# Sample attention in a two-layer encoder step: scores and values of two samples in one TensorE visit, new-key products last

## The chip, the core and the metric

The kernel runs on one core of one Trainium2 chip. The metric is the device time of one execution in microseconds (us); of several executions the median counts. Engines are named as the profile names them: PE is TensorE, PEld its weight loads, DVE is VectorE, ACT is ScalarE, POOL is GpSimd, SP is SyncE (here only a queue that issues transfers).

## What is computed

A two-layer trunk runs over 640 frames of width 1024: 512 frames of one prompt and 8 running samples of 16 new frames each. Each layer is a feed-forward half step, a mixer, and another feed-forward half step; all matrix products are in 32-bit accuracy. The mixer projects to convolution, attention and gate columns and joins two branches. The part that matters here is the attention of the samples: each of the 8 samples has 16 queries, 256 cached keys and 16 new ones, in 8 heads of 64.

```python
def _sample_attention(q, k, v, ck, cv, rel_bias):
    k_all = jnp.concatenate([ck, k], axis=1)
    v_all = jnp.concatenate([cv, v], axis=1)
    ...
    out = _band_attention(q, k_all, v_all, q_pos, k_pos, rel_bias)

def _band_attention(q, k, v, q_pos, k_pos, rel_bias):
    s = jnp.einsum('bqhd,bkhd->bhqk', q, k).astype(jnp.float32) * (HEAD_DIM ** -0.5)
    s = s + rel_bias[:, idx].astype(jnp.float32)[None]
    ...
    p = jax.nn.softmax(s, axis=-1).astype(v.dtype)
    return jnp.einsum('bhqk,bkhd->bqhd', p, v)
```

## The kernel before, in words

**The order of work on TensorE in a mixer is written out by hand.** `attention` (L1569) first makes the values of all frames, then queries and keys of a head pair. From there on the rest of the projection is a stream of steps (`work`, L1601): three more query/key pairs, the convolution columns, and the first pair of gate columns. `fill(n)` (L1606) takes the next n steps of that stream. A step is six products of 128 weights by 320 frames (`block`, L389, called in halves by `seven`, L698); fourteen steps make one pair of column blocks, and they use up four weight slabs. The attention's own products are put between such steps, so that TensorE has projection products to do while other engines work on the attention. One such insertion is called a visit here. The prompt's attention comes first (`scores`, L1646, `values`, L1689), then the samples'. On VectorE, ScalarE, GpSimd and the DMA queues the compiler's scheduler orders the instructions; those inside `soon()` (L365) get a higher priority.

**Weights** come in loads of 512 KB on SyncE's queue (L245). Each slab is split into a high part by ScalarE (`whi`, L305) and a low part by VectorE (`wlo`, L310), some slabs after sums of two blocks (L249), about two slabs ahead of TensorE. There are three buffers each of raw weights, high and low parts.

**Scores of a sample** (`sscores`, L1740): the cached keys are loaded in two halves (L1746, 256 KB each) and the cached values in one piece (L1749, 512 KB); GpSimd adds the new keys behind the cached ones (L1754). Four products (L1757), one for a pair of heads, put the scores into the four 32-row strips of one PSUM bank `spss`. They contract over 128 rows and yield 32 rows by 272 keys; the trace lists each product as two records with shape 128*32. VectorE adds the bias and takes the maximum into the tile `box` (L1764, tile `ss` in the trace), and `softmax` (L1821) negates the maximum on VectorE, takes exponentials on ScalarE and the reciprocal on VectorE.

**Values of a sample** (`svalues`, L1772) go in three parts. First, three transposes turn the weights, two of 128 columns for the cached keys and one of 16 columns for the new keys (L1780, L1781, bank `sptp`); ScalarE and VectorE copy them back into `box` (L1783, L1784). Second, the products with the values (L1791, bank `spy`): four with the 16 new keys (shape 16*32), then eight with the cached ones (128*32), each listed as two records; ScalarE scales the result into `box` (L1793). Third, one transpose turns the result into a shared bank `ptx` (L1797); when four samples are in it (`G = 4`), VectorE and ScalarE copy it out (L1803).

**Buffers.** `box`, the loaded keys, the loaded values and the new values have two buffers each, so those of sample b + 2 come free when sample b is through with them: keys after its scores, values after its value products, `box` after its result's turn. The PSUM banks of the attention are four (`att`, L209); the projection's own are four others.

**The loop over samples** (L1807 to L1819): scores of samples 0 and 1 in one visit; then for each sample 4 steps, the weights' turn, 3 steps, the scores of sample b + 2 and right behind them the values of sample b in one visit, 2 steps, the result's turn. That is 72 steps, all that the stream has left, and what follows is the next stage.

Of the kernel before, what the change touches and what calls it, by code (L numbers as in the profile page):

```python
# [12 lines left out]
AF = mybir.ActivationFunctionType  # L13
# [3 lines left out]
P = 128  # L17
D = 1024
L = 2
SEQ = 512  # L20
NB = 8
TS = 16
T = SEQ + NB * TS
HT = T // 2
PAST = 256
H = 8
HD = 64
# [153 lines left out]
def trunk(ctx: ExitStack, tc: tile.TileContext, xin, wst, small, pbias, samplebias, kcache, vcache,  # L181
          yout, ko, vo, co):
    nc = tc.nc
    PE, DVE, ACT, POOL, SP = nc.tensor, nc.vector, nc.scalar, nc.gpsimd, nc.sync
# [8 lines left out]
    ps = ExitStack()  # L193
# [15 lines left out]
    def att(name):  # L209
        return banks["att"].tile([P, 512], F32, tag="att", name=name)  # L210
# [15 lines left out]
    for kind, inside in kinds():  # L226
        n = len(fourth)
# [137 lines left out]
    def soon():  # L365
        return tc.high_priority(offset=300)
# [34 lines left out]
    ident = cp.tile([P, P], F32, name="ident")  # L401
# [12 lines left out]
    for k in range(KT):  # L414
# [4 lines left out]
        if k % 2 == 0:  # L419
            c = slice(k * P, (k + 2) * P)  # L420
# [693 lines left out]
    def mixer(l, after):  # L1114
        with tc.tile_pool(name=f"yp{l}", bufs=1, reuse_waits="tile") as yp, \
# [19 lines left out]
            with tc.tile_pool(name=f"mp{l}", bufs=2, reuse_waits="tile") as mp:  # L1135
# [63 lines left out]
                with tc.manual_schedule(engines={mybir.EngineType.PE}):  # L1199
                    attention(l, h, st, stats, ops, mp, yas, ycp, both, others())  # L1200
# [368 lines left out]
    def attention(l, h, norms, stats, ops, mp, yas, ycp, both, others):  # L1569
# [3 lines left out]
        npair = H // 2  # L1573
        nt = T // P
        NQ = SEQ // P
        KS = PAST + TS
# [29 lines left out]
        def fill(n):  # L1606
            for _ in range(n):
                next(stream, None)
# [5 lines left out]
        for c in range(KT // 2):  # L1614
            wh, wl = chunk()
            for kk in range(2):
# [3 lines left out]
                for t in range(nt):  # L1620
                    for j, (w, xx) in enumerate(((wh, xh), (wh, xl), (wl, xh))):
                        PE.matmul(pv[t], xx[:, t * P : (t + 1) * P],  # L1622
                                  w[:, kk * AW : (kk + 1) * AW],
                                  start=c == 0 and kk == 0 and j == 0,
                                  stop=c == KT // 2 - 1 and kk == 1 and j == 2)
# [63 lines left out]
        def values(p):  # L1689

            pt = [mp.tile([P, offs[-1] + SEQ], F32, name=f"pt{l}_{2 * p + e}", tag="pt") for e in range(2)]
            at = [sum(P * (NQ - i) for i in range(j)) for j in range(NQ)]

            def turn(j, e):
                w = (NQ - j) * P
                s = weights[2 * p + e]
                ptp = att(f"ptp{l}_{2 * p + e}_{j}")[:, :w]
                for i in range(j, NQ):
                    PE.transpose(ptp[:, (i - j) * P : (i - j + 1) * P],
                                 s[:, offs[i] + j * P : offs[i] + (j + 1) * P], ident)  # L1700
                with soon():
                    (ACT.copy if e else DVE.tensor_copy)(pt[e][:, at[j] : at[j] + w], ptp)

            for j in range(NQ):
                for e in range(2):
                    turn(j, e)
                if j % 2:
                    yield
            py = att(f"py{l}_{p}")
            for j in range(NQ):  # L1710
                for e in range(2):
                    hh = 2 * p + e
                    PE.matmul(py[e * HD : (e + 1) * HD, j * P :], vs[j][:, hh * HD : (hh + 1) * HD],
                              pt[e][:, at[j] : at[j] + (NQ - j) * P], start=j == 0, stop=j == NQ - 1)
            ACT.copy(yas[:, p, 0:SEQ], py)
            yield
# [5 lines left out]
        for p in range(npair):  # L1722
# [3 lines left out]
            vals = values(p)  # L1726
# [7 lines left out]

        sbias = mp.tile([P, KS], F32, name=f"sbias{l}", bufs=1)
        POOL.dma_start(sbias, samplebias[l])
        G = 4
        held, ptx = {}, [None]

        def sscores(b):  # L1740
            n = f"{l}_{b}"
            kcs = []
            for e, tag in enumerate("qk"):
                kc = mp.tile([P, T], F32, name=f"kc{n}_{e}", tag=tag)
                kcs.append(kc[:, : npair // 2 * KS].rearrange("p (a k) -> p a k", k=KS))
                SP.dma_start(kcs[e][:, :, :PAST], kcache[l, b, :, e * npair // 2 : (e + 1) * npair // 2])  # L1746
            vraw = mp.tile([P, offs[-1] + SEQ], F32, name=f"vc{n}", tag="s")
            vraw = vraw[:, : 2 * AW].rearrange("p (a k) -> p a k", a=2)
            SP.dma_start(vraw, vcache[l, b])  # L1749
            rows = slice(b * TS, (b + 1) * TS)  # L1750
            vn = mp.tile([P, SEQ], F32, name=f"vn{n}", tag="bias")[:TS, :AW]
            SP.dma_start(vn, vnew[rows])
            for e, kc in enumerate(kcs):
                POOL.tensor_copy(kc[:, :, PAST:], ks[:, e * npair // 2 : (e + 1) * npair // 2, rows])  # L1754
            pss = att(f"spss{n}")[:, :KS]
            for p in range(npair):
                PE.matmul(pss[32 * p : 32 * p + 32], bd[:, b, p, :], kcs[2 * p // npair][:, p % (npair // 2), :],  # L1757
                          start=True, stop=True)

            box = mp.tile([P, offs[-1] + SEQ], F32, name=f"ss{n}", tag="pt")  # L1760
            s = box[:, :KS]
            st = mp.tile([P, 4, NQ], F32, name=f"sst{n}", tag="st", bufs=4)
            with soon():
                DVE.tensor_tensor_reduce(out=s, in0=pss, in1=sbias, scale=1.0, scalar=NEG,  # L1764
                                         op0=ALU.add, op1=ALU.max, accum_out=st[:, 0, 0:1])

                softmax(s, st, [(0, KS)])
                if b == NB - 1:
                    ACT.activation(early, st[:, 3, 0:1], AF.Sigmoid)
            held[b] = box, st, vraw, vn  # L1770

        def svalues(b):  # L1772
            n = f"{l}_{b}"
            box, st, vraw, vn = held[b]
            s = box[:, :KS]
            pt = box[:, KS : KS + 2 * P].rearrange("p (a b) -> p a b", a=2)
            pn, yx = (box[:n, KS + o * P : KS + (o + 1) * P] for n, o in ((TS, 2), (P, 3)))
            ptp = att(f"sptp{n}")
            for j in range(2):
                PE.transpose(ptp[:, j * P : (j + 1) * P], s[:, j * P : (j + 1) * P], ident)  # L1780
            PE.transpose(ptp[:TS, 2 * P : 3 * P], s[:, PAST:], ident)  # L1781
            with soon():
                ACT.copy(pt, ptp[:, : 2 * P].rearrange("p (a b) -> p a b", a=2))  # L1783
                DVE.tensor_copy(pn, ptp[:TS, 2 * P : 3 * P])  # L1784
            yield

            pys = att(f"spy{n}")[:, :P]
            for j, (w, v) in enumerate(((pn, vn), (pt[:, 0], vraw[:, 0]), (pt[:, 1], vraw[:, 1]))):
                for p in range(npair):
                    r = slice(32 * p, 32 * p + 32)  # L1790
                    PE.matmul(pys[r], w[:, r], v[:, p * P : (p + 1) * P], start=j == 0, stop=j == 2)  # L1791
            with soon():
                ACT.activation(yx, pys, AF.Copy, scale=st[:, 3, 0:1])  # L1793
            yield
            if b % G == 0:
                ptx[0] = att(f"ptx{n}")
            PE.transpose(ptx[0][:, (b % G) * P : (b % G + 1) * P], yx, ident)  # L1797
            if b % G == G - 1:
                c0 = SEQ + (b + 1 - G) * TS
                for e in range(2):  # L1800
                    r = slice(e * HD, (e + 1) * HD)
                    with soon():
                        (ACT.copy if e else DVE.tensor_copy)(  # L1803
                            yas[r, :, c0 : c0 + G * TS].rearrange("p a (b t) -> p a b t", b=G),
                            ptx[0][r].rearrange("p (b a e t) -> p a b e t", b=G, a=npair, e=2)[:, :, :, e, :])

        sscores(0)  # L1807
        sscores(1)
        for b in range(NB):
            vals = svalues(b)  # L1810
            fill(4)
            next(vals)
            fill(3)
            if b + 2 < NB:
                sscores(b + 2)
            next(vals)
            fill(2)
            next(vals, None)
        fill(KT * KT)  # L1819

    def softmax(s, st, parts):  # L1821


        n = len(parts)
        with soon():
            DVE.tensor_scalar(out=st[:, 1, :n], in0=st[:, 0, :n], scalar1=-1.0, scalar2=None, op0=ALU.mult)
        for i, (o, w) in enumerate(parts):
            ACT.activation(s[:, o : o + w], s[:, o : o + w], AF.Exp, bias=st[:, 1, i : i + 1],
                           accum_out=st[:, 2, i : i + 1])
        with soon():  # L1830
            DVE.reciprocal(st[:, 3, :n], st[:, 2, :n])
# [294 lines left out]
```

## Time and profile before

| | us |
|---|---|
| median of 3 runs | 2496.21 |
| lowest and highest | 2496.2 and 2496.61 |
| the profiled execution | 2496.66 |
| its span, first to last instruction | 2494.7 |
| sample stage of layer 0, first scores to last result's turn | 562.07 to 642.63 |
| the same of layer 1 | 1795.10 to 1875.72 |

The mean granted TensorE clock is 0.998 of full speed. The sample stages are some 81 us each, so both together are 6% of the span. The page's first part gives busy time and share of the span by engine, its second part the span in 40 slices; the timeline gives single instructions with start and length. A record's length on TensorE contains its way through the array, so records overlap, and the pace is read from start to start.

### The profile page before, as it was taken

To read this page: it belongs to the slowest core of one execution; us is meant where nothing else is said; L and a number is where in the kernel's file an instruction comes from. 1 tells how busy PE (TensorE), PEld (TensorE's weight loads), DVE (VectorE), ACT (ScalarE), POOL (GpSimd) and SP (SyncE) were. 2 spreads that over 40 slices of the span, in tenths; PEclk is the share of its full clock that TensorE was granted. 3 is DMA by queue.
4 is the path that set the end of the run, shared out by engine and by line. 5 is a ranking of instruction groups with operands and counts; after the bars stand their busy time and mean duration, and the time that the engine had idled before them with its cause. 6 is when DMAs were issued, how large, how long until landed. Compare 5 with 4: busy or idle time off the path is not lost.

```text
span 2494.7 us, 43515 instructions
## 1 busy us (share of the span) xinstructions
PE 2478.1 (99%) x17048; PEld 2419.0 (97%) x17048; DVE 2119.2 (85%) x3322; ACT 1450.0 (58%) x2343; POOL 370.7 (15%) x445
## 2 busy tenths in 40 slices
PE   9999999999999999999999999999999999999998
PEld 8999999888999999999999999998899999999998
DVE  7888888878888899888798889888788888989887
ACT  7455556674666555555565555556646665555554
POOL 0011211211111011111001111221111110111111
PEclk9999999999999999999999999999999999999999
DMA  4245665335345344655435555643344553455554
GB/s 146 82 107 124 138 135 130 106 115 167 99 119 145 101 116 118 138 135 135 117 90 126 129 134 123 138 119 115 125 153 104 126 141 95 119 133 122 129 135 110
DMA packets 133261, 308.10 MB, mean 124 GB/s; under 512 B 12768, under 2 KB 76128, under 8 KB 133056
## 3 DMA queue, kind: packets, MB, share of 16 engines
q1 hardware_dynamic: 68976, 219.18, 27.3%
q0 software_dynamic: 63360, 85.50, 20.6%
q8 instruction: 133, 2.18, 0.4%
q10 hardware_dynamic: 720, 0.65, 0.1%
q14 instruction: 72, 0.59, 0.1%
HBM read 221.13 MB, written 7.94 MB: 92 GB/s over the span
## 4 chain that ended last, share of the span: by engine, by line
PE 94%; DVE 3%; ACT 2%; DMA 1%; issue 0%; SPq 0%; DVEq 0%; ACTq 0%
PE pab L395 12%; PE paa L395 11%; PE pcb L395 6%; PE pca L395 6%; PE daa L962 5%; PE dab L962 5%; PE po L372 4%; PE qa L395 4%; PE pbb L395 3%; PE pba L395 3%; PE dca L962 3%; PE dcb L962 3%; PE pda L372 2%; PE pv L1622 2%; PE ma_cv L395 2%; PE qc L395 2%
## 5 line engine op out<-in xcount | busy, mean ns | idle before, releaser
L310 DVE TENSOR_TENSOR wlo<-raw,whi 128x512 fp32r<-128x512 f32 (+1 forms) x583 | 598.6, 1030 | 236.1 <-ACT whi L305 230.6
L305 ACT CAST whi<-raw 128x512 fp32r<-128x512 f32 (+1 forms) x583 | 519.9, 897 | 348.0 <-PE pbb L395 44.6
L305 ACT CAST whi<-s 128x1024 fp32r<-128x1024 f32 (+1 forms) x164 | 153.6, 937 | 248.1 <-issue 107.8
L395 PE MATMUL pab<-xhib,whi 128*128 128x320 f32 x704 | 218.3, 310 | 0.4 <-DVE gb L249 0.4
L395 PE MATMUL pab<-xhib,wlo 128*128 128x320 f32 x704 | 217.4, 309 | 0.0
L395 PE MATMUL pab<-xlob,whi 128*128 128x320 f32 x704 | 217.4, 309 | 0.0
L395 PE MATMUL paa<-xhia,whi 128*128 128x320 f32 x640 | 198.0, 309 | 0.2 <-DVE ga L249 0.2
L395 PE MATMUL paa<-xloa,whi 128*128 128x320 f32 x640 | 197.6, 309 | 0.0
L395 PE MATMUL paa<-xhia,wlo 128*128 128x320 f32 x640 | 197.6, 309 | 0.0
L310 DVE TENSOR_TENSOR wlo<-s,whi 128x1024 fp32r<-128x1024 f32 (+1 forms) x164 | 176.6, 1077 | 10.4 <-ACT whi L305 10.4
L395 PEld LDWEIGHTS pab<-xhib,whi 128*128 128x128 f32 x704 | 132.2, 188 | 1.1 <-DVE gb L249 0.9
L395 PEld LDWEIGHTS pab<-xlob,whi 128*128 128x128 f32 x704 | 132.2, 188 | 0.2
L395 PEld LDWEIGHTS pab<-xhib,wlo 128*128 128x128 f32 x704 | 132.2, 188 | 0.0
L395 PEld LDWEIGHTS paa<-xhia,whi 128*128 128x128 f32 x640 | 120.2, 188 | 0.5 <-DVE ga L249 0.5
L395 PEld LDWEIGHTS paa<-xloa,whi 128*128 128x128 f32 x640 | 120.2, 188 | 0.1
L395 PEld LDWEIGHTS paa<-xhia,wlo 128*128 128x128 f32 x640 | 120.2, 188 | 0.0
L249 DVE TENSOR_TENSOR raw<-raw,raw 128x512 f32<-128x512 f32 x164 | 112.2, 684 | 1.8 <-DMA raw<-in_wst 0.2
L249 DVE TENSOR_TENSOR raw<-s,raw 128x512 f32<-128x512 f32 x164 | 112.3, 685 | 0.0
L395 PE MATMUL pcb<-xhib,whi 128*128 128x320 f32 x352 | 108.7, 309 | 0.0
L395 PE MATMUL pcb<-xlob,whi 128*128 128x320 f32 x352 | 108.7, 309 | 0.0
L395 PE MATMUL pcb<-xhib,wlo 128*128 128x320 f32 x352 | 108.7, 309 | 0.0
L986 POOL DMA_DIRECT2D x<-c_b x52 | 62.6, 1203 | 309.5 <-ACT c_b L979 134.5
(816 smaller groups left out, 8170.8 us busy)
## 6 DMA issues: line engine op xcount, KB each, us to landing
raw<-in_wst SPq DMA_DIRECT2D x375, 512.0 KB, 3.7
x<-c_b POOLq DMA_DIRECT2D x52, 320.0 KB, 5.1
x<-c_a POOLq DMA_DIRECT2D x50, 320.0 KB, 5.0
kc<-in_kcache SPq DMA_DIRECT2D x32, 256.0 KB, 4.1
vc<-in_vcache SPq DMA_DIRECT2D x16, 512.0 KB, 4.5
ub<-cbb POOLq DMA_DIRECT2D x42, 160.0 KB, 5.9
ua<-cba POOLq DMA_DIRECT2D x38, 160.0 KB, 5.4
x<-u_a POOLq DMA_DIRECT2D x18, 320.0 KB, 5.1
```

Of the source, the lines that this page charges most:

```text
L249: DVE.tensor_tensor(out=out, in0=a, in1=b, op=ALU.add)
L305: ACT.copy(hi[:, d], src[:, c])
L310: DVE.tensor_tensor(out=lo, in0=src, in1=hi.bitcast(F32), op=ALU.subtract)
L372: PE.matmul(ps[a] if isinstance(ps, list) else ps[:, a, :HT], w, x[:, a * HT : (a + 1) * HT], start=first and j == 0, stop=last and j == 2)
L395: PE.matmul(ps, a, b, start=start and kp == 0 and j == 0, stop=stop and kp == NP - 1 and j == 2, skip_group_check=True)
L962: PE.matmul(ps[u], w, y, start=start and i == 0 and j == 0, stop=i == 1 and j == 2, skip_group_check=True)
L986: POOL.dma_start(rows(r, cols), z, accum_op=ALU.add)
L1622: PE.matmul(pv[t], xx[:, t * P : (t + 1) * P], w[:, kk * AW : (kk + 1) * AW], start=c == 0 and kk == 0 and j == 0, stop=c == KT // 2 - 1 a ...
```

## The change

Samples are taken two by two. `svalues` takes a pair: it turns the weights of both in one visit; then the cached-value products of both come first and the products with the 16 new keys of both come last; then both results are turned in one visit and copied out at once (`G = 2`). In the loop, the scores of the next two samples stand right ahead of this pair's values. The steps between are 7 behind the first scores, then for each pair 4 between weights' turn and values, 4 between values and results' turn, and 10 before the next pair; three steps of the stream remain for the last `fill`. The products themselves are the same.

```diff
-        G = 4
+        G = 2
...
-        def svalues(b):
...
+        def svalues(bs):
+            boxes = [held[b][0] for b in bs]
...
+            for b, box, pt, pn in zip(bs, boxes, pts, pns):
+                s = box[:, :KS]
+                ptp = att(f"sptp{l}_{b}")
+                for j in range(2):
+                    PE.transpose(ptp[:, j * P : (j + 1) * P], s[:, j * P : (j + 1) * P], ident)
+                PE.transpose(ptp[:TS, 2 * P : 3 * P], s[:, PAST:], ident)
+                with soon():
+                    ACT.copy(pt, ptp[:, : 2 * P].rearrange("p (a b) -> p a b", a=2))
+                    DVE.tensor_copy(pn, ptp[:TS, 2 * P : 3 * P])
             yield
...
-            pys = att(f"spy{n}")[:, :P]
-            for j, (w, v) in enumerate(((pn, vn), (pt[:, 0], vraw[:, 0]), (pt[:, 1], vraw[:, 1]))):
-                for p in range(npair):
-                    r = slice(32 * p, 32 * p + 32)
-                    PE.matmul(pys[r], w[:, r], v[:, p * P : (p + 1) * P], start=j == 0, stop=j == 2)
-            with soon():
-                ACT.activation(yx, pys, AF.Copy, scale=st[:, 3, 0:1])
+            pys = [att(f"spy{l}_{b}")[:, :P] for b in bs]
+            for js in ((0, 1), (2,)):
+                for b, ps, pt, pn in zip(bs, pys, pts, pns):
+                    vraw, vn = held[b][2:]
+                    for j in js:
+                        w, v = (pn, vn) if j == 2 else (pt[:, j], vraw[:, j])
+                        for p in range(npair):
+                            r = slice(32 * p, 32 * p + 32)
+                            PE.matmul(ps[r], w[:, r], v[:, p * P : (p + 1) * P], start=j == 0, stop=j == 2)
+            for b, ps, yx in zip(bs, pys, yxs):
+                with soon():
+                    ACT.activation(yx, ps, AF.Copy, scale=held[b][1][:, 3, 0:1])
             yield
...
+            for b, yx in zip(bs, yxs):
+                if b % G == 0:
+                    ptx[0] = att(f"ptx{l}_{b}")[:, : G * P]
+                PE.transpose(ptx[0][:, (b % G) * P : (b % G + 1) * P], yx, ident)
+                if b % G == G - 1:
...
         sscores(0)
         sscores(1)
-        for b in range(NB):
-            vals = svalues(b)
+        fill(7)
+        for b in range(0, NB, 2):
+            vals = svalues((b, b + 1))
+            next(vals)
             fill(4)
+            for c in range(b + 2, min(b + 4, NB)):
+                sscores(c)
             next(vals)
-            fill(3)
-            if b + 2 < NB:
-                sscores(b + 2)
-            next(vals)
-            fill(2)
+            fill(4)
             next(vals, None)
+            fill(10 if b + 2 < NB else 0)
         fill(KT * KT)
```

More of the change, by code (lines that the diff above doesn't have):

```diff
@@ L1770, in sscores @@
             held[b] = box, st, vraw, vn
-        def svalues(b):
[L1773 to L1781, printed above, removed]
-            with soon():
-                ACT.copy(pt, ptp[:, : 2 * P].rearrange("p (a b) -> p a b", a=2))
-                DVE.tensor_copy(pn, ptp[:TS, 2 * P : 3 * P])
-            yield
-            pys = att(f"spy{n}")[:, :P]
-            for j, (w, v) in enumerate(((pn, vn), (pt[:, 0], vraw[:, 0]), (pt[:, 1], vraw[:, 1]))):
-                for p in range(npair):
-                    r = slice(32 * p, 32 * p + 32)
-                    PE.matmul(pys[r], w[:, r], v[:, p * P : (p + 1) * P], start=j == 0, stop=j == 2)
-            with soon():
-                ACT.activation(yx, pys, AF.Copy, scale=st[:, 3, 0:1])
-            yield
[L1795 to L1805, printed above, removed]
@@ new lines, in svalues @@
+        def svalues(bs):
+            boxes = [held[b][0] for b in bs]
+            pts = [z[:, KS : KS + 2 * P].rearrange("p (a b) -> p a b", a=2) for z in boxes]
+            pns, yxs = ([z[:n, KS + o * P : KS + (o + 1) * P] for z in boxes] for n, o in ((TS, 2), (P, 3)))
+            for b, box, pt, pn in zip(bs, boxes, pts, pns):
[7 more added lines that the diff above has]
+                    DVE.tensor_copy(pn, ptp[:TS, 2 * P : 3 * P])
+            yield
+            pys = [att(f"spy{l}_{b}")[:, :P] for b in bs]
[10 more added lines that the diff above has]
+                    ACT.activation(yx, ps, AF.Copy, scale=held[b][1][:, 3, 0:1])
+            yield
+            for b, yx in zip(bs, yxs):
[3 more added lines that the diff above has]
+                if b % G == G - 1:
+                    c0 = SEQ + (b + 1 - G) * TS
+                    for e in range(2):
+                        r = slice(e * HD, (e + 1) * HD)
+                        with soon():
+                            (ACT.copy if e else DVE.tensor_copy)(
+                                yas[r, :, c0 : c0 + G * TS].rearrange("p a (b t) -> p a b t", b=G),
+                                ptx[0][r].rearrange("p (b a e t) -> p a b e t", b=G, a=npair, e=2)[:, :, :, e, :])
```

## The prediction

> **What bounds the kernel now.** I read the first lines of the profile's page first, then the chain of work that ended last, then the table of busy time by stretch for the sample stage, then TensorE's own timeline in that stage.
>
> ```profile
> span 2494.7 us, 43515 instructions
> ...
> PE 2478.1 (99%) x17048; PEld 2419.0 (97%) x17048; DVE 2119.2 (85%) x3322; ACT 1450.0 (58%) x2343; POOL 370.7 (15%) x445
> ...
> PE 94%; DVE 3%; ACT 2%; DMA 1%; issue 0%; SPq 0%; DVEq 0%; ACTq 0%
> ...
> 562.00:643.00 81.00, 81.00 (x723) 72.67 (x723) 66.38 (x142) 41.20 (x84) 10.03 (x23) 1.00 0.45 147
> ```
>
> TensorE is 94% of the chain that ended last. The last row is layer 0's sample stage: TensorE busy 81.00 of 81.00 us, VectorE 66.38, ScalarE 41.20, granted clock 1.00. So TensorE never idles there, and the stage ends sooner only if TensorE needs fewer microseconds for the same products. But a busy TensorE isn't one at its pace: its records overlap. So I measure by starts, not by durations. These are the timeline's rows (start, length, engine, line, names, shape, count) at the five kinds of visit that the attention pays amid the projection's steps:
>
> ```profile
> 561.83 0.31 PE L395 MATMUL mc_cv<-hhim,wlo 128*128 128x320 f32 x1
> 562.07 1.12 PE L1757 MATMUL spss<-kc,bd 128*32 128x272 f32 x16
> 563.12 0.41 PE L395 MATMUL ma_cv<-thi,whi 128*128 128x320 f32 x1
> 563.38 0.31 PE L395 MATMUL ma_cv<-tlo,whi 128*128 128x320 f32 x1
> ...
> 564.99 0.30 PE L395 MATMUL ma_b<-hhim,whi 128*128 128x320 f32 x1
> ...
> 566.60 0.32 PE L395 MATMUL ma_b<-hhim,wlo 128*128 128x320 f32 x1
> 566.75 0.38 PE L1780 MATMUL sptp<-ident,ss 128*128 128x128 f32 x2
> 566.97 0.27 PE L1781 MATMUL sptp<-ident,ss 128*16 128x128 f32 x1
> 567.00 0.39 PE L395 MATMUL mb_b<-hhim,whi 128*128 128x320 f32 x1
> 567.23 0.30 PE L395 MATMUL mb_b<-hlom,whi 128*128 128x320 f32 x1
> ...
> 569.58 0.31 PE L395 MATMUL ma_b<-thi,wlo 128*128 128x320 f32 x1
> 569.81 0.67 PE L1757 MATMUL spss<-kc,bd 128*32 128x272 f32 x8
> 570.41 0.42 PE L1791 MATMUL spy<-vn,ss 16*32 16x128 f32 x8
> 570.76 0.64 PE L1791 MATMUL spy<-vc,ss 128*32 128x128 f32 x16
> 571.34 0.42 PE L395 MATMUL ma_b<-thi,whi 128*128 128x320 f32 x1
> 571.59 0.31 PE L395 MATMUL ma_b<-tlo,whi 128*128 128x320 f32 x1
> ...
> 573.05 0.31 PE L395 MATMUL mc_b<-hhim,wlo 128*128 128x320 f32 x1
> 573.20 0.27 PE L1797 MATMUL ptx<-ident,ss 128*128 128x128 f32 x1
> 573.22 0.39 PE L395 MATMUL mc_b<-hhim,whi 128*128 128x320 f32 x1
> 573.45 0.31 PE L395 MATMUL mc_b<-hlom,whi 128*128 128x320 f32 x1
> ...
> 639.61 0.31 PE L395 MATMUL mc_g<-hhim,wlo 128*128 128x320 f32 x1
> 639.85 0.42 PE L1791 MATMUL spy<-vn,ss 16*32 16x128 f32 x8
> 640.20 0.65 PE L1791 MATMUL spy<-vc,ss 128*32 128x128 f32 x16
> 640.77 0.41 PE L395 MATMUL ma_g<-thi,whi 128*128 128x320 f32 x1
> 641.02 0.31 PE L395 MATMUL ma_g<-tlo,whi 128*128 128x320 f32 x1
> ```
>
> The pace of the projection: the twelve products from 564.99 to 566.60 are 1.61 us over 11 gaps, 0.146 each; a step of the filler stream is six of them, 0.88 us. A visit's price is the time from the last projection start before it to the second one after it, less two gaps (0.29). First scores (two samples): 1.55 - 0.29 = 1.26. Turning one sample's weights: 0.63 - 0.29 = 0.34. Scores and values together: 2.01 - 0.29 = 1.72. Values alone: 1.41 - 0.29 = 1.12. Turning one result: 0.40 - 0.29 = 0.11. A layer pays 1.26 + 8 x 0.34 + 6 x 1.72 + 2 x 1.12 + 8 x 0.11 = 17.4 us, both layers 34.8. Nothing beyond a part of this can be won.
>
> Where it goes inside a visit: 16 score records take 1.05 us to the next start, 8 take 0.60 (569.81 to 570.41), so 8 cost 0.45 and 0.15 is a tail paid once, when the shape in the timeline changes (128*32 to 16*32, or back to 128*128). Of the values, 16 cached records take 0.58 and 8 of 16 keys 0.35, each followed by a change of shape: at one pace that is 0.225 per 8 records and a tail of 0.125. Entering costs 0.23 instead of 0.146, and the gap after leaving is 0.25 instead of 0.146: 0.19 for going in and out.
>
> **The change, part by part.** (a) *Scores and values in pairs, 16-key products last.* No product is added or removed; the visits become three per layer with 16 scores, 32 cached and 16 new-key records, and one without scores. The new visit: scores 0.90, no change of shape to the cached products, these 4 x 0.225 = 0.90 with a tail of 0.125, the new keys 2 x 0.225 with a tail of 0.125, and 0.19 for in and out: 2.69. Two old ones were 3.44, so 0.75 is saved: by terms one in-and-out of 0.19, two tails from scores to new keys, 0.30, and two of the four tails of values, 0.25. The last pair: 0.90 + 0.125 + 0.45 + 0.125 + 0.19 = 1.79 against 2.24, 0.45 saved. Per layer 3 x 0.75 + 0.45 = 2.70, **both layers 5.4 us**.
>
> What the trace doesn't show: scores directly before cached products, equal in shape but unequal in length and target. Bounds: nothing, as between the first visit's two samples, which run through in one pace, or the full tail of 0.15, as before the new keys; six places, 0 to 0.9 us. I take nothing, the nearest row having the same shape on both sides. The Trainium skill, page "TensorEngine Tiling (Array Packing)", section "Key Properties", has it that changing the tiling mode drains TensorE and changing only the tile doesn't; by that the sum would be the 5.4 that I take, and the opposite reading would leave 4.5; the trace agrees so far as its tails stand only where the shape changes. Second unknown: 16 new-key records in a row. If the 0.35 were all pace and no tail, they would cost 0.70 and not 0.575, 1.0 us more over eight visits; if the tail is the scores' 0.15, 0.2 less. I take the pace of the cached ones.
>
> (b) *Turning in pairs.* Six transposes in one visit instead of three twice. The start-to-start of two transposes is 0.11 (566.75 to 566.97, two of them), and a lone one costs 0.11 as well (573.05 to 573.45), so each costs its own pace and the visit is free: nothing saved. Unknown is a full transpose behind the 16-column one: 0.03 (as 566.97 to 567.00) to a tail of 0.15 beyond pace, over eight pairs -0.6 to +1.2; I take the pace, as nothing in 566.97 to 567.23 looks unlike 573.20 to 573.45. The results' turns in twos: nothing, by the same rows.
>
> (c) *Result copies by two samples, not four.* Two more copies per layer on VectorE and ScalarE each, at most 0.41 and 0.37 us apiece as the larger ones now take. VectorE has 81.00 - 66.38 = 14.6 us free there, so nothing; without that cover 1.6 us at most.
>
> (d) *New places among the steps.* The filler steps are 7 + 4 x 8 + 3 x 10 = 69 instead of 72, and three run behind the last turn: the same products, no price. Each wait's cover, at 0.88 us a step, against the rows that answer:
>
> ```profile
> 567.28 0.38 ACT L1783 COPY ss<-sptp 128x256 f32<-128x256 f32 x1
> 571.47 0.37 ACT L1793 ACTIVATE ss<-spy,sst 128x128 f32<-128x128 f32 x1 [1.91 <-PE spy L1791]
> 573.51 0.44 DVE L1764 CUSTOM_DVE_ANT_0 ss<-spss,sbias 128x272 f32<-128x272 f32 x1 [1.06 <-PE ptx L1797]
> 577.69 0.68 DVE L249 TENSOR_TENSOR raw<-raw,raw 128x512 f32<-128x512 f32 x1
> ...
> 584.46 0.69 DVE L310 TENSOR_TENSOR wlo<-raw,whi 128x512 fp32r<-128x512 f32 x1 [0.34 <-ACT whi L305]
> 585.16 0.31 PE L395 MATMUL ma_cv<-thi,whi 128*128 128x320 f32 x1
> ...
> 562.76 8.16 SPq L1746 DMA_DIRECT2D kc<-in_kcache  x5
> 571.03 0.41 SPq L245 DMA_DIRECT2D raw<-in_wst  x1
> ...
> GB/s 6 276 236 8 49 325 316 348 22 43 260 240 3 150 340 237 295 28 11 67 250 344 354 37 19 232 55 0 247 259 239 53 8 0 0 0 283 233 2 8
> ...
> kc<-in_kcache SPq DMA_DIRECT2D x12, 256.0 KB, 4.6
> vc<-in_vcache SPq DMA_DIRECT2D x6, 512.0 KB, 5.0
> ```
>
> Turns to values: now four steps, 3.5 us (2.6 before), for two copies of 0.38. Values to the result's turn: four steps for two of 0.37 (two steps before). Result's turn to the next pair's turn, in which both score reduces, negations and exponentials lie: ten steps, 8.8 us. Score reduces wait for the result's turn as now (the third row: VectorE stood 1.06 us), because a sample's tile comes free there; two now stand at that place, behind them on VectorE the low halves of the weights. Keys of the next two samples: 1 MB, four loads of 4.6 us that overlap, issued after one visit for the next, 18 steps or 15.9 us later. I cost (d) at nothing.
>
> Sum: 5.4 us of the profiled execution, span 2494.7 to 2489.3. That execution took 2496.66, 2.0 beyond its span, and lies 0.45 over the median 2496.21; carried to the median, **2490.8**.
>
> **The rivals.** *The tails are saved only in part* (a drain between scores and cached values, or dear new keys): what speaks for it is that no row shows these neighbours; against, that equal shapes run through in the first visit. One of the two full costs gives 5.4 - 0.9 = 4.5 or 4.4: 2491.8.
>
> *The bunching costs waits.* Two samples' copies, reduces and exponentials now come at once, ahead of weight halves on VectorE and ScalarE. For it: at 584.46 a low half ended at 585.15, and TensorE began on that slab at 585.16; against: it began with the slab's other half, and TensorE waited nowhere in the stage. A wait of 0.45 us at each of six visits takes half the gain: 2493.5. Beside this stands a rule of the Trainium skill, "TensorEngine Tiling (Array Packing)", section "PSUM Bottleneck": when tiling has sped up TensorE, emptying PSUM can become the bound; the trace so far doesn't bear it out, as ScalarE had stood 1.91 us when the values came.
>
> *The weights' loads get stuck behind the keys* (the slow side). SyncE's queue is in order: the five key loads took 8.16 us to issue, since the fifth waited for sample 2's scores, and the weight load at 571.03 stood behind it. Those scores move from 569.8 to about 573.6 (first visit's end 563.1, eleven steps, a turn), 3.8 us later, and four key loads instead of one may lie ahead, 0.75 MB or 2.1 us at the 354 GB/s that this stage's fullest slices show in the GB/s row above. The load would come 5.9 us later. If it takes the 5.0 of a load of the same size (the values'), it landed at 576.0, and VectorE first read it at 577.69: 1.7 us of cover. From there it decides; 4.2 us at six visits are 25.2: 2496.2 - 5.4 + 25.2 = 2516.0. Against: nothing ties this load to the keys but the order in which they were written to the queue, and with the visit later it can as well be issued ahead of them.
>
> *Cheaper still*: the 16-column transpose hidden and the new keys quicker, 5.4 + 0.6 + 0.2 = 6.2: 2490.0.
>
> **How the numbers follow.** Forecast 2490.8 (2490.3 to 2491.2): 0.46. In part 2491.8: 0.20. Waits 2493.5: 0.20. Stuck loads 2516.0: 0.06. Cheaper 2490.0: 0.08. A measurement of this kernel can tell about 0.2% from no change, 5.0 us, so faster means below 2491.2 and slower above 2501.2. Faster: nearly all of the forecast and the cheaper case, 0.52; slower 0.06; within 0.42. The range from 2489.8 to 2494.8 leaves out the stuck loads, the worse end of the waits and a little below the cheaper case.
>
> **What would show it.** In the profile after: the pair visits cost 2.7 us by the same measure, with one start-to-start of about 0.23 between the last scores and the first cached products; visits of turns 0.66 to 0.68; the stage from first scores to last result's turn, with three steps (2.6 us) fewer, about 5.3 us shorter per layer; TensorE without waits. A tail of 0.34 between scores and cached values, TensorE waiting for a weight half, or VectorE waiting for a weight load in this stage would show me wrong, and so would a change of time outside the two stages.

## The result, and the profile after

| | before | after |
|---|---|---|
| median of 22 runs each, us | 2496.62 | 2493.64 |
| ratio, with its 95% interval | | 0.9988 (0.9983 to 0.9994) |
| the profiled execution, us | 2496.66 | 2494.42 |
| its span, us | 2494.7 | 2492.6 |
| sample stage, layer 0 and layer 1, us | 80.82 and 80.88 | 79.36 and 79.36 |

The kernel is 2.98 us (0.12%) faster: inside the range on record, and little more than half of the 5.4 us forecast. The sample stage is taken here from the first score product to the second product of the next stage. It is 1.46 and 1.52 us shorter, together 2.98 us, so the whole result lies in the two stages. (The profiled spans differ by only 2.1 us because the profiled execution after was 0.85 us late before its first sample stage, at 562.92 instead of 562.07; the profiles of this case reach that point between 561.77 and 562.92.)

The page's first lines after, and the row of busy time for layer 0's sample stage, stand against those of before that the prediction shows:

```profile
span 2492.6 us, 43527 instructions
...
PE 2474.3 (99%) x17048; PEld 2422.4 (97%) x17048; DVE 2120.3 (85%) x3326; ACT 1450.7 (58%) x2347; POOL 365.1 (15%) x445
```

```profile
562.50:643.00 80.50, 79.47 (x730) 74.62 (x729) 66.60 (x145) 41.44 (x86) 7.15 (x23) 1.00 0.44 148
```

TensorE was busy 81.00 of 81.00 us before; now 79.47 of 80.50: it idles 1.03 us in the stage. The table of TensorE's waits over the whole execution (line, whom it waited for, us in all, times, longest) names the place:

```profile
PE poa L372 <- ACT whi L618: 5.7, 1, 5.7
PE mc_b L395 <- ACT c L728: 2.1, 2, 1.0
```

The first row is at the kernel's start and was there before (5.6). The second is new: once in each layer. First, though, the visits themselves. The timeline after shows one turn of a pair's weights, one pair visit with scores, and the last one without:

```profile
570.09 0.31 PE L395 MATMUL ma_b<-thi,wlo 128*128 128x320 f32 x1
570.24 0.38 PE L1780 MATMUL sptp<-ident,ss 128*128 128x128 f32 x2
...
570.81 0.39 PE L395 MATMUL ma_b<-thi,whi 128*128 128x320 f32 x1
571.04 0.31 PE L395 MATMUL ma_b<-tlo,whi 128*128 128x320 f32 x1
...
574.27 0.31 PE L395 MATMUL ma_b<-thi,wlo 128*128 128x320 f32 x1
574.51 1.12 PE L1757 MATMUL spss<-kc,bd 128*32 128x272 f32 x16
575.45 1.06 PE L1795 MATMUL spy<-vc,ss 128*32 128x128 f32 x32
576.43 0.64 PE L1795 MATMUL spy<-vn,ss 16*32 16x128 f32 x16
577.00 0.42 PE L395 MATMUL ma_b<-thi,whi 128*128 128x320 f32 x1
577.26 0.31 PE L395 MATMUL ma_b<-tlo,whi 128*128 128x320 f32 x1
...
633.82 0.31 PE L395 MATMUL mc_g<-hhim,wlo 128*128 128x320 f32 x1
634.06 1.08 PE L1795 MATMUL spy<-vc,ss 128*32 128x128 f32 x32
635.07 0.64 PE L1795 MATMUL spy<-vn,ss 16*32 16x128 f32 x16
635.64 0.41 PE L395 MATMUL mc_g<-hhim,whi 128*128 128x320 f32 x1
635.89 0.30 PE L395 MATMUL mc_g<-hlom,whi 128*128 128x320 f32 x1
```

Read as before, from the last projection start ahead to the second one behind, less two gaps of 0.147: the pair's turn costs 0.95 - 0.29 = 0.66, the pair visit 2.99 - 0.29 = 2.70 (forecast 2.69), the last 2.07 - 0.29 = 1.78 (forecast 1.79). The 16 score records take 0.94 to the first cached product, not the 1.05 that they take to a product of another shape in the first visit: no tail, as assumed. (The sum of 2.69 met 2.70 with some luck in its terms: the scores take 0.04 more than the 0.90 put in, the cached products 0.98 and not 1.025.) Over all 25 visits of a layer before and 13 after, the same measure adds up to 34.76 us before and 29.23 after in both layers: **the visits gave 5.5 us.** Here is what took 2.6 us of it back, first TensorE's timeline, then ScalarE's:

```profile
620.56 0.31 PE L395 MATMUL ma_b<-thi,whi 128*128 128x320 f32 x1
...
622.18 0.30 PE L395 MATMUL ma_b<-thi,wlo 128*128 128x320 f32 x1
623.51 0.42 PE L395 MATMUL mc_b<-hhim,whi 128*128 128x320 f32 x1 [1.03 <-ACT c L728]
623.76 0.31 PE L395 MATMUL mc_b<-hlom,whi 128*128 128x320 f32 x1
```

```profile
620.65 1.05 ACT L305 CAST whi<-raw 128x1024 fp32r<-128x1024 f32 x1 [1.44 <-PE mc_b L395]
621.61 0.52 ACT L1835 ACTIVATE ss<-ss,sst 128x272 f32<-128x272 f32 x1
622.03 0.19 ACT L1835 ACTIVATION_READ_ACCUMULATOR ss<-ss,sst 128x1 f32 x1
622.12 0.51 ACT L1835 ACTIVATE ss<-ss,sst 128x272 f32<-128x272 f32 x1
622.54 0.19 ACT L1835 ACTIVATION_READ_ACCUMULATOR ss<-ss,sst 128x1 f32 x1
622.75 0.26 ACT L1809 COPY ya<-ptx 64x128 f32<-64x128 f32 x1
623.03 0.43 ACT L728 COPY c<-mc_b 128x320 f32<-128x320 f32 x1
```

In the projection's fourteen steps the bank `mc` gets a first sum in steps 7 and 8 and is added to in steps 11 and 12; between the two, ScalarE must copy the first sum out (L728). So it has the two steps in between, 1.76 us. TensorE began them at 620.56 and would have gone on at about 622.3. The third pair's results are turned between steps 7 and 8. That turn releases the exponentials of the last two samples and a copy of the results, and these three stand ahead of the partial-sum copy on ScalarE, behind a weight cast. The copy starts at 623.03 and TensorE goes on at 623.51. The start-to-start of 1.33 and the slow gap of 0.25 behind it are 1.29 us more than two gaps: 2 x 1.29 = 2.6 us. 5.5 - 2.6 = 2.9, against 2.98 measured.

### The profile page after: what moved, and what is told of

It reads as the page before. It is cut to its first block, busy times and chain, and to the rows that moved or that the text cites. A ratio compares the mean times of both kernels' runs of the same rounds, so it can differ in the third digit from the quotient of the medians.

```text
span 2492.6 us, 43527 instructions
## 1 busy us (share of the span) xinstructions
PE 2474.3 (99%) x17048; PEld 2422.4 (97%) x17048; DVE 2120.3 (85%) x3326; ACT 1450.7 (58%) x2347; POOL 365.1 (15%) x445
## 4 chain that ended last, share of the span: by engine, by line
PE 94%; DVE 3%; ACT 2%; issue 0%; DMA 0%; SPq 0%; DVEq 0%; ACTq 0%
PE pab L395 12%; PE paa L395 11%; PE pcb L395 6%; PE pca L395 6%; PE daa L962 5%; PE dab L962 5%; PE qa L395 4%; PE po L372 4%; PE pbb L395 3%; PE pba L395 3%; PE dcb L962 3%; PE dca L962 3%; PE poa L372 2%; PE pda L372 2%; PE pv L1622 2%; PE ma_cv L395 2%
```

## The experiments

**Theory A:** the wait comes because the pair's two exponentials and result copy stand on ScalarE ahead of the partial-sum copy, at this place of the projection. **Rival B:** the weight cast ahead of them, which waited 1.44 us for its buffer, makes it late. **Rival C:** it belongs to the third pair as such, whose successors are the last samples. In the expectations a stage is measured from one projection start earlier to two products later than in this document, 0.54 us more (79.90 there for 79.36).

**The third pair's results turned later.** The edit, in the loop of the changed kernel:

```diff
-            fill(4)
+            fill(7 if b == 4 else 4)
             next(vals, None)
-            fill(10 if b + 2 < NB else 0)
+            fill((7 if b == 4 else 10) if b + 2 < NB else 0)
```

> The changed kernel with the third pair's result turn three steps later (7 steps ahead of it, 7 behind it, instead of 4 and 10). Theory A (the changed kernel's one wait of TensorE per layer comes because the pair's two exponentials and the result copy stand on ScalarE ahead of the copy of a projection partial sum): the turn now falls behind that copy, no wait in either layer, each sample stage 1.3 us shorter than in the changed kernel, and the whole 5.5 us below the kernel before. Rival B (the weight cast that waits for its buffer ahead of that copy makes it late): the cast is still ahead, a wait of about 1 us per layer stays, 3.0 us below the kernel before. Rival C (something of the third pair itself, such as the last samples' sigmoid preparation): a wait stays near that pair, wherever its turn is.

Measured: 2491.73, ratio 0.9980 (0.9971 to 0.9989); stages 78.55, 0.81 shorter than after, not 1.3. The wait for the partial sum is gone, though the cast still stands ahead of the copy: that speaks against B and C. But a smaller wait came, at the next weights' turn. TensorE's and VectorE's timelines of this kernel:

```profile
629.76 0.30 PE L395 MATMUL ma_g<-tlo,whi 128*128 128x320 f32 x1
630.23 0.41 PE L395 MATMUL ma_g<-thi,wlo 128*128 128x320 f32 x1 [0.17 <-DVE wlo L310]
```

```profile
629.22 0.27 DVE L1784 COPY ss<-sptp 16x128 f32<-16x128 f32 x1
629.48 0.69 DVE L310 TENSOR_TENSOR wlo<-s,whi 128x512 fp32r<-128x512 f32 x1
```

The first product with a low half starts at 630.23, just after VectorE had made that half (629.48 and 0.69), behind the copy of the turned weights; with the gaps around it 0.47 us are lost. So the move showed that the place decides, and wasn't free itself.

**The second pair's results turned at the same place.** The edit is alike, `fill(8 if b == 2 else 4)` and `fill((6 if b == 2 else 10) if b + 2 < NB else 0)`.

> The changed kernel with the second pair's result turn four steps later (8 steps ahead, 6 behind), so that it falls at the same place of the projection's fourteen steps as the third pair's does. Theory A: a second wait of the same kind per layer, on the same partial-sum copy of the earlier column pair, about 1.0 us of idle and 1.3 us of stage; the whole 2.6 us slower than the changed kernel, about 0.4 us below the kernel before. Rival C (the third pair is special): no new wait, 3.0 us below the kernel before. Rival B: a second wait only if a weight cast stands there too.

Measured: 2496.62, ratio 0.9999 (0.9989 to 1.0008); stages 80.64, 1.28 longer than after. The waits of layer 0's stage:

```profile
PE mc_cv L395 <- ACT c L728: 1.0, 1, 1.0
PE mc_b L395 <- ACT c L728: 1.0, 1, 1.0
```

The same wait, now twice. It is the place that makes it, not the pair: C falls, and two such waits per layer eat the whole gain of the pairs. (A weight cast of 1.05 us stands ahead here too, so B needs the next run.)

**The partial-sum copy put first on ScalarE.** TensorE's order is the changed kernel's, and the weight cast stays where it is. The edit holds for every such copy: in the profile five copies per layer stand earlier in ScalarE's order, the one in question, another of the projection (L716) some 6 us behind it and three in the prompt's attention, and VectorE's order differs at a few places behind the copy in question.

```diff
         yield from mul(pc, s, 1, X["T5"], True)
-        with soon():
+        with tc.high_priority(offset=900):
             ACT.copy(c5, pc)
```

> The changed kernel with nothing moved on TensorE; only the copy of that partial sum has a higher priority, so that on ScalarE it stands ahead of the third pair's exponentials and behind the same weight cast. Theory A: no wait, stages 1.3 us shorter, 5.5 us below the kernel before, as in the kernel with the later turn. Rival B (the cast): the wait stays at about 1 us, 3.0 us below the kernel before.

Measured: 2490.75, ratio 0.9976 (0.9966 to 0.9985); stages 78.08, 1.28 shorter than after. ScalarE and TensorE of this kernel at the same place:

```profile
620.13 1.05 ACT L305 CAST whi<-raw 128x1024 fp32r<-128x1024 f32 x1 [1.44 <-PE mc_b L395]
621.09 0.42 ACT L728 COPY c<-mc_b 128x320 f32<-128x320 f32 x1
621.40 0.53 ACT L1835 ACTIVATE ss<-ss,sst 128x272 f32<-128x272 f32 x1
```

```profile
621.66 0.31 PE L395 MATMUL ma_b<-thi,wlo 128*128 128x320 f32 x1
621.80 0.31 PE L395 MATMUL mc_b<-hhim,whi 128*128 128x320 f32 x1
```

The cast is still ahead, idle for 1.44 us before it as in the changed kernel; the copy ends at 621.51, and TensorE passes from 621.66 to 621.80 at its usual pace. The cast alone doesn't make the wait: B falls as the whole cause, and A holds. The cast is part of the sum all the same, 0.96 of the 2.38 us ahead of the copy. An estimate from the rows after: without the cast, the exponentials and the result copy (1.42 us) and the copy itself would let TensorE go on at about 622.55, only some 0.2 us late; that was not tried. The time is close to the 2490.8 that was forecast, and this version is faster than both kernels of the case.

**Control: that priority in the kernel before.** The same edit.

> The kernel before with only the higher priority of the partial-sum copy, as a control for the run that had it in the changed kernel. Theory A (the priority helps only by the wait that the pairs had made): no change, as TensorE has no wait there before; stages 81.4 us, 2496.7 us in all. If the priority helps by itself: up to 2.6 us below the kernel before.

Measured: 2496.50, ratio 0.9999 (0.9990 to 1.0008); stages 80.82 and 80.86. In the sample stages it changed no order on ScalarE; it moved three copies per layer in the prompt's attention, the same three as in the changed kernel, and that gave nothing.

**The order inside the visit turned back,** in the changed kernel:

```diff
-            for js in ((0, 1), (2,)):
+            for js in ((2,), (0, 1)):
...
-PE.matmul(ps[r], ..., start=j == 0, stop=j == 2)
+PE.matmul(ps[r], ..., start=j == 2, stop=j == 1)
```

> The changed kernel with the order of the products inside a pair's visit turned back: the 16-key products of both samples first, then the cached ones. If a tail is paid where the shape changes: one tail of about 0.14 us more (0.11 and a slower second group of 0.02) in each of the three visits per layer that hold scores, 2.83 us a visit instead of 2.69, and nothing in the fourth visit (1.78); 0.8 us slower than the changed kernel in both layers. If the gain of a visit comes from pairing alone: 2.69 us a visit. The wait on the partial sum is not touched and stays.

Measured: 2494.11, ratio 0.9988 (0.9979 to 0.9997), where 0.5 us more than after can't be told from none; but stages 79.80, 0.44 longer than after. Its timeline:

```profile
573.88 1.12 PE L1757 MATMUL spss<-kc,bd 128*32 128x272 f32 x16
574.93 0.64 PE L1795 MATMUL spy<-vn,ss 16*32 16x128 f32 x16
575.50 1.08 PE L1795 MATMUL spy<-vc,ss 128*32 128x128 f32 x32
576.51 0.42 PE L395 MATMUL ma_b<-thi,whi 128*128 128x320 f32 x1
```

Scores now take 1.05 to the next group (0.94 after) and the cached products 1.01 (0.98): 2.63 from the first score to the projection instead of 2.49, which makes 2.83 a visit as expected. The wait on the partial sum stayed, 1.0 us in each layer.

**The order alone, without pairs,** in the kernel before:

```diff
-for j, (w, v) in enumerate(((pn, vn), (pt[:, 0], vraw[:, 0]), (pt[:, 1], vraw[:, 1]))):
+for j, (w, v) in enumerate(((pt[:, 0], vraw[:, 0]), (pt[:, 1], vraw[:, 1]), (pn, vn))):
```

> The kernel before, samples still one by one, with one edit: in a sample's values the products with the cached keys come first and the 16-key products last. If the tail belongs to the change of shape: in the six visits per layer that hold scores the tail between scores and the next products goes, 1.58 us a visit instead of 1.72, nothing in the two others (1.12); 1.65 us less in both layers, 0.07% below the kernel before, no wait of TensorE in the stage. If it belongs to the change of target or length: 1.72 us a visit, no change.

Measured: 2494.96, ratio 0.9991 (0.9982 to 1.0000), an interval that just reaches no change; stages 79.98 and 80.03, 0.84 and 0.85 shorter than before. Its timeline:

```profile
570.14 0.67 PE L1757 MATMUL spss<-kc,bd 128*32 128x272 f32 x8
570.62 0.62 PE L1791 MATMUL spy<-vc,ss 128*32 128x128 f32 x16
571.17 0.42 PE L1791 MATMUL spy<-vn,ss 16*32 16x128 f32 x8
571.52 0.42 PE L395 MATMUL ma_b<-thi,whi 128*128 128x320 f32 x1
```

1.38 from the first score to the projection instead of 1.53 before. So of the 5.5 us that the visits gave, 1.7 need only a new order and no wait comes with them; the other 3.8 come from pairing.

**The last tail taken away too:** the kernel with the partial-sum copy first, with the new keys' products widened to 128 rows by zeros.

```diff
-vn = mp.tile([P, SEQ], F32, name=f"vn{n}", tag="bias")[:TS, :AW]
-SP.dma_start(vn, vnew[rows])
+vn = mp.tile([P, SEQ], F32, name=f"vn{n}", tag="bias")[:, :AW]
+POOL.memset(vn, 0.0)
+SP.dma_start(vn[:TS], vnew[rows])
...
+POOL.memset(box[:, KS + 2 * P : KS + 3 * P], 0.0)
...
-    DVE.tensor_copy(pn, ptp[:TS, 2 * P : 3 * P])
+    DVE.tensor_copy(pn[:TS], ptp[:TS, 2 * P : 3 * P])
```

> The kernel with the partial-sum copy first, and the new keys' products widened to 128 rows: GpSimd writes zeros over the rows behind the 16 keys in the turned weights and in the new values, so that the whole values' visit has the shape 128*32. If the remaining tail inside a visit belongs to the change from 128 to 16 rows, it goes: 2.56 us a pair visit instead of 2.69, 1.64 instead of 1.78 in the last, each sample stage 0.55 us shorter (78.06 instead of 78.61), 1.1 us below the kernel with the copy first and 7.1 us below the kernel before. If the tail belongs to the switch between groups of products as such: no change in the visits. A GpSimd fill that comes late would show as a wait of TensorE or of SyncE's queue.

Measured: 2490.97, ratio 0.9978 (0.9969 to 0.9987); stages 77.60, 0.48 shorter than with the copy first. Its timeline at a pair visit:

```profile
574.43 1.12 PE L1758 MATMUL spss<-kc,bd 128*32 128x272 f32 x16
575.37 1.06 PE L1797 MATMUL spy<-vc,ss 128*32 128x128 f32 x32
576.24 0.62 PE L1797 MATMUL spy<-vn,ss 128*32 128x128 f32 x16
576.79 0.41 PE L395 MATMUL ma_b<-thi,whi 128*128 128x320 f32 x1
```

2.36 instead of 2.49: the tail goes with the change of shape, as expected. But by the medians the whole is no faster than with the copy first. TensorE's waits for the prompt attention's copies (`ptp`, ahead of the sample stages) were 1.6 us in this profile and 0.7 in the other; that could take back 0.9 of the 1.0 us, but isn't shown to, for the two profiled spans still differ by 0.7 us (2489.0 and 2489.7). The two were not measured side by side, and why those waits grew was not tried; whether this version is worth its two fills stays open.

## Why the prediction came out as it did

*What bounds.* Right. TensorE was the stage's bound to the end: what was taken from its visits, less its waits, came off the whole (2.95 us by the two measures, 2.98 measured). Only in the last run, with 128 rows, the medians don't show the stages' further 1.0 us.

*(a) Pairs, new keys last.* Right: 2.70 and 1.78 measured for 2.69 and 1.79, and no tail between scores and cached products. The two unknowns fell on the side taken. In the runs with the 16-row group moved or widened, a tail of some 0.14 us comes or goes with each change of shape, and where the number of changes stays the same, so does the price (1.12 in the visits without scores). The Trainium skill, "TensorEngine Tiling (Array Packing)", section "Key Properties", has it that a change of tiling mode drains TensorE and a change of tile doesn't; the runs agree with it by those 0.14 us.

*(b) Turns, (c) copies.* (b) is right: 0.66 for a pair's turn as for two single ones. (c) was put at nothing for VectorE's free time; but the third pair's result copy, which the kernel before didn't make at that turn, is one of the pieces ahead of the partial-sum copy on ScalarE, 0.28 of the 2.38 us.

*(d) New places among the steps, "I cost (d) at nothing".* **This is the step that failed.** I gave each of the attention's own waits its cover in steps and found them covered; they were, TensorE never waited for one. I didn't ask the reverse: which projection work on ScalarE falls due just when the pair's exponentials come in a bundle. A partial sum has two steps to be copied out, 1.76 us, and the cast, two exponentials with their sums and a result copy ahead of it take 2.4 us. A single exponential before did no harm. At one place it stood with the cast ahead of that copy, here ScalarE and then TensorE of the kernel before:

```profile
605.02 0.52 ACT L1828 ACTIVATE ss<-ss,sst 128x272 f32<-128x272 f32 x1
605.54 1.03 ACT L305 CAST whi<-raw 128x1024 fp32r<-128x1024 f32 x1
606.60 0.43 ACT L728 COPY c<-mc_cv 128x320 f32<-128x320 f32 x1
607.33 0.39 PE L395 MATMUL mc_cv<-hhim,whi 128*128 128x320 f32 x1
```

The copy ended at 607.03, 0.30 us ahead of the product that needed it. That is less than a second exponential takes (0.51).

*The rivals.* "The bunching costs waits" (2493.5, chance 0.20) is the case that came, at 2493.64, but not by its working. I put 0.45 us at six visits on the low halves of weights, 2.7 us; it was 1.29 us at two places, on a partial sum. That both come to 2.6 or 2.7 us, and so that time to the one measured, is luck. The low half was the victim only in the run with the later turn, with 0.47 us. In the sample stage TensorE waited nowhere for the attention's own banks; it waited for the projection's bank, which the same ScalarE had to empty (1.03 us of idle). The other rule that I weighed, the Trainium skill's "TensorEngine Tiling (Array Packing)", section "PSUM Bottleneck", says that copying out of PSUM may become the bound once tiling has sped up TensorE. The runs show something narrower: one copy was late by its place in the order, for the wait went when that copy was put first, with ScalarE making the same copies. Stuck loads did not come: no wait of TensorE in the stage leads to a load.

*The numbers.* The forecast was 0.46 likely; its time is about what the kernel takes once the wait is gone (2490.75). That it meets it to 0.1 us is in part luck: the forecast counts 5.4 us from 2496.21, while beside that run the kernel before took 2496.71, 6.0 us more, of which the two stages hold 5.5. The result lies within 0.2% of before, a case that I gave 0.42. Two of the signs named went against the forecast: TensorE had a wait, and from first scores to last result's turn the stage got 4.1 us shorter (80.56 to 76.45), not 5.3, which is that wait.

## What to carry to other kernels

Where small products interrupt a long stream on TensorE, count the changes of shape and group the products by shape; here a change costs about 0.14 us and going in and out of the stream 0.19. When work of two items is bundled, don't only check that the bundle is covered: look at what the helper engines owe the main stream within the same microseconds, above all sums that must leave PSUM before TensorE adds to the same bank, and put those ahead in the queue. Moving the bundle to another step may only find the next victim; the order on the one engine settled it.

## What the runs showed of the hardware

A wait costs TensorE more than its idle time: 1.03 us idle was 1.29 us lost, since the wait hides how early the next product would have started and the gap behind it is 0.25 instead of 0.147. Widening the new keys' products from 16 rows to 128 cost nothing in itself: 16 records took 0.55 us to the next group with 128 rows and 0.57 with 16. And a transpose in a row of transposes costs 0.11 us start to start though its record lasts 0.27, so a pair of turns in one visit costs as much as in two.
